# A second FFN with seven block products, GpSimd's queue for the block sums of the last FFN, and a chunk split from its head in the third FFN

## The chip, the cores and the metric

The kernel runs on one core of one Trainium2 chip. The metric is device time in microseconds (us). Every run has a time of its own; one execution was also recorded by the hardware profiler, and its span, from the first to the last instruction, is a little shorter than its time.

## What is computed

The reference is a trunk of two layers for 256 tokens of width 1024, in float32. Each layer is an FFN, a mixer and a second FFN, each behind an RMSNorm and added to the stream:

```python
def swiglu(x, w_gate, w_up, w_down):
    return (jax.nn.silu(x @ w_gate) * (x @ w_up)) @ w_down
...
        h = h + 0.5 * swiglu(rms_norm(h, ffn1_norm[layer]),
                             ffn1_w_gate[layer], ffn1_w_up[layer], ffn1_w_down[layer])
        hn = rms_norm(h, mix_norm[layer])
...
        h = h + 0.5 * swiglu(rms_norm(h, ffn2_norm[layer]),
                             ffn2_w_gate[layer], ffn2_w_up[layer], ffn2_w_down[layer])
    return rms_norm(h, final_norm)
```

There are four FFNs, 1024 wide outside and 2816 inside. The mixer of the first layer is dilated attention beside a gated MLP, that of the second is block-sparse attention; the change does not touch them.

## The kernel before

**Stages.** The work runs in six phases: FFN (phase 0), mixer (1), FFN (2), FFN (3), mixer (4), FFN (5). "First FFN" below is phase 0, "second" phase 2, "third" phase 3, "last" phase 5.

**A product is three matmuls.** Each float32 operand is split into a high part (rounded to the matmul's format) and a low part (the rest); `mm3` (lines 387 to 390) multiplies high by high, high by low and low by high. ACT makes the high part of a weight (`whi`, line 249), DVE the low part (`wlo`, line 256).

**Weights come in chunks.** `weight_chunks()` lists them in the order of use, mostly 1 MB: eight 128-row tiles of 256 columns. Class `Stream` loads them on SP's DMA queue into three buffers `raw` (line 201), splits them into four buffers `whi`/`wlo` and hands them to PE. So DVE and ACT can be at most four chunks ahead of PE: a chunk's split can begin when PE has left the chunk four places before it. A chunk with `reset=RESET` is split from a small head (the first three tiles, in two pieces of 384 columns) instead of in two halves of 1024.

**An FFN.** For each of 11 pairs of hidden tiles PE works one gate chunk and one up chunk, 48 matmuls each. Then `gated` (line 717) forms the hidden values: DVE multiplies the gate bank by the norm's row (`gs`, line 720), ACT takes the SiLU, DVE multiplies by the up bank (`hm`, line 723), and ACT and DVE split the result into `hTh` and `hTl` (line 393). Nothing can be gated until `everywhere` (lines 476 to 493) has summed the squares (`mean`, a square root on ACT, a reciprocal on DVE, `row`). The down projection follows: four groups of 256 output columns, each of three chunks (8, 8 and 6 tiles); `Next.pair` (line 430) takes a group out of its bank: `part` (437), `x` (438), then the split of the stream for the next phase, `xTh` and `xTl` (427).

**Seven products.** In the first FFN (`woven`) the first 512 columns of the down projection are made by seven block products instead of eight: the 256x256 block of hidden values and the 256x512 block of weights of a pair are cut in quarters, sums of quarters are formed, and `seven_products` (line 748) runs 7 x 3 matmuls on one chunk of kind "S" (0.5 MB). The sums of hidden quarters (`f` in `gated`, lines 738 to 740, split into `hSh` and `hSl`) and of weight quarters (lines 263, 266 and 267) are DVE's. They are worked `LAG` = 4 pairs behind the gating; the last four stand in the down projection. `gather_first` adds the seven results up, and `turned` (line 782) turns them round by four PE transposes for each 256 columns.

**Sums for the last FFN.** The last FFN uses the same trick with nine of its down chunks. Their weight sums are made early, in the second and third FFN, by `begin_sums` (line 657): fetch 1 MB from HBM into a buffer `blocks` (line 666), form the sums in place on DVE (lines 670 to 672, and 676 into `block` for five of them), write 1 MB (or 1 MB and 256 KB) back to HBM (line 682). Both transfers are issued by SP, in its queue behind the last weight load. `AHEAD` names the chunks (phase, n) after which a fetch is issued; the sums are issued one chunk later and the write two chunks later. There are two `blocks` buffers.

**The order.** Each engine has one instruction queue, worked in order. The order is fixed when the program is built by a scheduler, which places an instruction where it expects its inputs to be there; `issue_after` ties an instruction to another of the same engine.

Of the kernel before, what the change touches and what calls it, by code (L numbers as in the profile page):

```python
# [10 lines left out]
F32 = mybir.dt.float32  # L11
F32R = mybir.dt.float32r
# [8 lines left out]
FT = FF // 128  # L21
# [3 lines left out]
CH = 2048  # L25
# [20 lines left out]
SPARE = 2  # L46
AHEAD = [(phase, n) for phase in (2, 3) for n in (4, 8, 12, 16)] + [(3, 19)]

WOVEN = (0,)
LAG = 4  # L50
MSHIFT, HSHIFT = 16, 56
# [4 lines left out]
def weight_chunks():  # L56
# [10 lines left out]

    def ffn(name, layer, last=False, again=(2, 3), woven=False):
        first = len(chunks)
        wd = (f"{name}_w_down", layer)  # L70

        def seven(pair):
            add(wd, pair * 256, 2, 0, 512, MSHIFT, kind="S")

        for c in range(0, FF, 256):
            if len(chunks) == 0:
                for k in (0, 4):
                    add((f"{name}_w_gate", f"{name}_w_up", layer), k * 128, 4, c, c + 256, SHIFT,
                        (1, 2, 3) if k else (0.5, 1, 1.5, 2, 3))
                continue  # L80
            for m in ("gate", "up"):
                n = len(chunks)
                cuts = (6,) if first == 0 and n in again else ()
                cols((f"{name}_w_{m}", layer), c, 256, cuts,
                     RESET if n - first in again or woven and m == "gate" and c // 256 > LAG else 0)
            if woven and c // 256 >= LAG:
                seven(c // 256 - LAG)
        if last:
            for i in range(FT // 2):
                add(wd, i * 256, 2, 0, D, kind=LAST[i])  # L90
            return
        rest = list(range(FT // 2 - LAG, FT // 2)) if woven else []
        behind = woven
        if woven:
            seven(rest.pop(0))
        for c in range(512 if woven else 0, D, 256):
            for k, n in DOWN:
                add(wd, k * 128, n, c, c + 256, SHIFT, reset=RESET if behind else 0)
                behind = bool(rest)
                if rest:  # L100
                    seven(rest.pop(0))
# [6 lines left out]

    ffn("ffn1", 0, again=(2,), woven=0 in WOVEN)
    wab = ("ab_w_in", 0)  # L110
# [6 lines left out]
    mix(("ab_w_out", 0), MIX1)  # L117
    ffn("ffn2", 0, again=(2,), woven=2 in WOVEN)
    ffn("ffn1", 1, again=(), woven=3 in WOVEN)
    wc = ("c_w_in", 0)  # L120
# [225 lines left out]
def trunk(ctx: ExitStack, tc: tile.TileContext, a, out):  # L346
# [311 lines left out]
    def begin_sums(fp, n):  # L658
# [4 lines left out]
        j = st.chunks - FT // 2 + i  # L663
        t = fp.tile([128, CH], F32, name="blocks", bufs=2)
        with tc.issue_after(st.last.ins):
            nc.sync.dma_start(t, st.weights[j].rearrange("(p c) -> p c", p=128))
        b22, b12, b11, b21 = (t[:, i * 512 : (i + 1) * 512] for i in range(4))

        def sums():
            nc.vector.tensor_sub(b12, b22, b12)  # L670
            nc.vector.tensor_add(b11, b12, b11)
            nc.vector.tensor_sub(b21, b11, b21)
            formed = [t]
            if LAST[i] == "X":
                formed.append(fp.tile([128, 512], F32, name="block", bufs=1))
                nc.vector.tensor_sub(formed[1], b11, b22)

            def keep():
                st.sums[j] = [dram.tile(list(b.shape), F32, name=f"blocks{n}{m}") for m, b in enumerate(formed)]
                with tc.issue_after(st.last.ins):  # L680
                    for to, b in zip(st.sums[j], formed):
                        nc.sync.dma_start(to, b)

            return keep
# [3 lines left out]
    def ffn(phase):  # L688
        nonlocal nxt
        with tc.tile_pool(name="fp", bufs=1) as fp:  # L690
            hT = [fp.tile([128, FT, S], F32R, name=n) for n in ("hTh", "hTl")]
            last = phase == 5
            woven = phase in WOVEN
            if last:
# [23 lines left out]
            def gated(k, pg, pu):  # L718
# [16 lines left out]
                if woven:  # L735
# [4 lines left out]
                    nc.vector.tensor_add(f[:, 3], a12, f[:, 2])  # L740
                    summed[k // 2] = [fp.tile([128, 4 * 128 + LINE], F32R, name=m, bufs=LAG + 1)[:, HSHIFT : HSHIFT + 512]
                                        .rearrange("p (i c) -> p i c", i=4) for m in ("hSh", "hSl")]
# [50 lines left out]
            for n in range(FT):  # L793
# [13 lines left out]
                if (phase, n) in AHEAD:  # L807
                    ahead.append(begin_sums(fp, AHEAD.index((phase, n))))
                if (phase, n - 1) in AHEAD:
                    ahead.append(ahead.pop()())  # L810
                if (phase, n - 2) in AHEAD:
                    ahead.pop()()
# [16 lines left out]
                elif n > late and m == 1:  # L829
                    gated(k, *ready[-2:])  # L830
                if woven and m == 1 and k // 2 >= LAG:
                    seven_products(k // 2 - LAG)
            if last:
# [6 lines left out]
            nxt = Next(phase + 1)  # L840
            rest = list(range(FT // 2 - LAG, FT // 2)) if woven else []
            if woven:
                seven_products(rest.pop(0))
            for c in range(2 if woven else 0, 4):
                b = bank()
                for k0, n in DOWN:
                    w = st.take()
                    turns = [(j, kk) for kk in range(RESET, n) for j in range(2)]
                    for j, kk in [(j, kk) for j in range(2) for kk in range(RESET)] + turns:
# [3 lines left out]
                            k == j == 0, k == FT - 1 and j == 1)  # L853
                        if woven and c == 3 and k0 == 8 and j and kk in (3, 6):
                            turned(kk // 6, quarters[kk // 6])
# [600 lines left out]
```

## Time and profile before

| | |
|---|---|
| median of 3 runs | 922.58 us (922.55 to 923.53) |
| the profiled execution's own time | 922.25 us |
| its span | 920.5 us |
| first FFN, to 187 us | PE busy 186.17, DVE 168.18, ACT 119.39 |
| second FFN, 272 to 453 us | PE busy 181.00, DVE 126.42, ACT 92.77 |
| third FFN, 453 to 632 us | PE busy 179.00, DVE 124.06, ACT 87.30 |

A page of the profile gives, for each engine, the busy time, its waits with what ended them, and the chain of work that ended last. PE's matmuls overlap: one lasts about 0.28 us but the next starts 0.113 us after it, so that a busy PE is read by the distance between starts. "Pitch" below is that distance, for DVE's instructions too.

### The profile page before, as it was taken

The page shows a single profiled execution, that of the slowest core. Times are in us where ns is not written, and L with a number is a line of the kernel's source. Part 1 is how long each engine was busy: PE and PEld are TensorE (multiplying, and loading weights), DVE is VectorE, ACT ScalarE, POOL GpSimd, SP SyncE. Part 2 cuts the span into 40 slices and gives each one's busy share as a digit, 9 for nine tenths or more (in the row PEclk, how much of TensorE's full clock was granted, in tenths as well). Part 3 has the DMA queues.
Part 4 walks back from the last instruction along what each step waited for, and adds up shares of the span by engine and source line. Part 5 has one row for each costly group of instructions (what it writes and reads, how often), then busy time and mean ns, then how long its engine had stood idle before and what let it go on. Part 6 is the DMA issues. An engine that isn't in the chain of part 4 may idle for free.

```text
span 920.5 us, 18362 instructions
## 1 busy us (share of the span) xinstructions
PE 912.8 (99%) x7558; PEld 894.0 (97%) x7558; DVE 730.7 (79%) x1162; ACT 545.3 (59%) x840; POOL 82.1 (9%) x117
## 2 busy tenths in 40 slices
PE   9999999999999999999999999999999999999997
PEld 9999999989999999999999999999999999999886
DVE  7999897997889767655786677666778799878896
ACT  7766555668667544444564454355776777555574
POOL 0000000034310000000000000001565100000002
PEclk9999999999999999999999999999999999999999
DMA  9646555665256777765557877855433566755681
GB/s 331 244 163 239 201 177 204 231 227 183 93 184 229 245 276 266 288 236 214 205 207 271 294 255 295 323 210 199 177 138 138 134 228 223 271 201 194 230 310 54
DMA packets 34707, 202.17 MB, mean 220 GB/s; under 512 B 3984, under 2 KB 6288, under 8 KB 13760
## 3 DMA queue, kind: packets, MB, share of 16 engines
q1 hardware_dynamic: 33120, 197.79, 60.1%
q0 software_dynamic: 496, 1.77, 0.9%
q10 hardware_dynamic: 1008, 1.44, 0.5%
q8 instruction: 59, 0.97, 0.4%
q14 instruction: 24, 0.20, 0.1%
HBM read 188.14 MB, written 12.85 MB: 218 GB/s over the span
## 4 chain that ended last, share of the span: by engine, by line
PE 94%; issue 4%; DVE 1%; POOL 0%; ACT 0%; POOLq 0%; DVEq 0%
PE bank L388 30%; PE bank L389 30%; PE bank L390 30%; PE bank L636 1%; PE bank L1158 1%; DVE wlo L256 1%; PE bank L612 0%; PE bank L639 0%; POOL xTl L902 0%; PE bank L1120 0%; ACT whi L249 0%; PE bank L1122 0%; DVE xTl L427 0%; PE bank L1121 0%; DVE x L438 0%
## 5 line engine op out<-in xcount | busy, mean ns | idle before, releaser
L249 ACT ACTIVATE whi<-raw 128x1024 fp32r<-128x1024 f32 (+5 forms) x369 | 341.6, 970 | 244.0 <-PE bank L389 125.2
L256 DVE TENSOR_TENSOR wlo<-raw,whi 128x1024 fp32r<-128x1024 f32 (+5 forms) x369 | 402.8, 1120 | 56.3 <-ACT whi L249 55.2
L388 PE MATMUL bank<-xTh,whi 128*128 128x256 f32 x1600 | 442.7, 277 | 0.0
L389 PE MATMUL bank<-xTl,whi 128*128 128x256 f32 x1600 | 441.9, 276 | 0.3 <-DVE xTl L427 0.3
L390 PE MATMUL bank<-xTh,wlo 128*128 128x256 f32 x1600 | 441.8, 276 | 0.0
L389 PEld LDWEIGHTS bank<-xTl,whi 128*128 128x128 f32 x1600 | 300.4, 188 | 0.6 <-DVE xTl L427 0.5
L388 PEld LDWEIGHTS bank<-xTh,whi 128*128 128x128 f32 x1600 | 300.4, 188 | 0.0
L390 PEld LDWEIGHTS bank<-xTh,wlo 128*128 128x128 f32 x1600 | 300.4, 188 | 0.0
L388 PE MATMUL bank<-hTh,whi 128*128 128x256 f32 x440 | 121.7, 277 | 0.0
L390 PE MATMUL bank<-hTh,wlo 128*128 128x256 f32 x440 | 121.5, 276 | 0.0
L389 PE MATMUL bank<-hTl,whi 128*128 128x256 f32 x440 | 121.5, 276 | 0.0
L389 PEld LDWEIGHTS bank<-hTl,whi 128*128 128x128 f32 x440 | 82.6, 188 | 0.0
L388 PEld LDWEIGHTS bank<-hTh,whi 128*128 128x128 f32 x440 | 82.6, 188 | 0.0
L390 PEld LDWEIGHTS bank<-hTh,wlo 128*128 128x128 f32 x440 | 82.6, 188 | 0.0
L723 DVE TENSOR_TENSOR hm<-gs,bank 128x512 f32<-128x512 f32 x44 | 29.9, 683 | 34.8 <-PE bank L390 34.6
L1053 POOL MEMSET k<- 64x256 f32 x12 | 3.2, 306 | 563.7 <-ACT whi L249 378.9
L720 DVE TENSOR_TENSOR gs<-bank,row 128x512 f32<-128x512 f32 x44 | 30.1, 685 | 14.0 <-PE bank L390 13.9
L388 PE MATMUL bank<-mixh,whi 128*128 128x256 f32 x128 | 35.7, 279 | 0.0
L1149 POOL TENSOR_SCALAR pr<-pr,rl 128x128 f32<-128x128 f32 (+1 forms) x36 | 33.1, 931 | 28.2 <-DVE rl L1145 19.2
L390 PE MATMUL bank<-mixh,wlo 128*128 128x256 f32 x128 | 35.4, 277 | 0.0
L389 PE MATMUL bank<-mixl,whi 128*128 128x256 f32 x128 | 35.4, 276 | 0.0
L393 ACT ACTIVATE hTh<-hm 128x512 fp32r<-128x512 f32 x44 | 27.2, 619 | 10.4 <-DVE hm L723 9.5
(247 smaller groups left out, 1149.4 us busy)
## 6 DMA issues: line engine op xcount, KB each, us to landing
raw<-in_weights SPq DMA_DIRECT2D x135, 1024.0 KB, 5.0
blocks<-in_weights SPq DMA_DIRECT2D x9, 1024.0 KB, 9.3
blocks<-blocks SPq DMA_DIRECT2D x9, 1024.0 KB, 9.0
raw<-in_weights SPq DMA_DIRECT2D x17, 512.0 KB, 3.5
raw<-in_weights SPq DMA_DIRECT2D x10, 768.0 KB, 6.3
raw<-blocks SPq DMA_DIRECT2D x7, 1024.0 KB, 4.8
raw<-in_weights SPq DMA_DIRECT2D x7, 256.0 KB, 4.7
blocks<-block SPq DMA_DIRECT2D x5, 256.0 KB, 8.7
```

The costliest lines, as they stand in the source:

```text
L249: done = nc.scalar.activation(hi, r, AF.Copy)
L256: self.made[u] = done, nc.vector.tensor_sub(lo, r, hi.bitcast(F32))
L388: nc.tensor.matmul(p, sh, mh, start=start, stop=False)
L389: nc.tensor.matmul(p, sh, ml, start=False, stop=False)
L390: return nc.tensor.matmul(p, sl, mh, start=False, stop=stop)
L393: return nc.scalar.activation(hi, src, AF.Copy), nc.vector.tensor_sub(lo, src, hi.bitcast(F32))
L636: nc.tensor.matmul(o, w[0][i][:, cs], xT[m][:, k], start=k == 0 and m == "h" and j % 2 == 0, stop=False)
L720: nc.vector.tensor_mul(g, both(pg), twice(norm["row"]))
L723: nc.vector.tensor_mul(hm, g, both(pu))
L1053: nc.gpsimd.memset(pair[j][o, 1].bitcast(F32), 0.0)
L1149: share = engine.tensor_scalar(pr[:, cs], pr[:, cs], rl[:, b : b + 1], None, op0=ALU.mult)
L1158: nc.tensor.transpose(tp[:, i * 128 : (i + 1) * 128], pr[:, i * 128 : (i + 1) * 128], ident)
```

## The change

It does five things:

1. `WOVEN` and `LAG` become `LAGS = {0: 4, 2: 2}`: the second FFN too makes its first 512 down columns by seven products, two pairs behind the gating. Its last two pairs stand in the down projection, and `turned` stands one down chunk earlier than in the first FFN.
2. `begin_sums` issues its fetch and its writes on GpSimd's queue instead of SP's.
3. There is one `blocks` buffer instead of two.
4. The sums are issued two chunks behind their fetch and the write three, from other places (`AHEAD`).
5. In the third FFN the second chunk (the first up chunk) is split from its head.

```diff
-AHEAD = [(phase, n) for phase in (2, 3) for n in (4, 8, 12, 16)] + [(3, 19)]
-
-WOVEN = (0,)
-LAG = 4
+AHEAD = [(2, n) for n in (3, 7, 11, 15)] + [(3, n) for n in (2, 6, 10, 14, 18)]
+
+LAGS = {0: 4, 2: 2}
...
-            if woven and c // 256 >= LAG:
-                seven(c // 256 - LAG)
+            if c // 256 >= lag:
+                seven(c // 256 - lag)
...
-        if woven:
+        if lag > 2 and woven:
             seven(rest.pop(0))
...
-    ffn("ffn2", 0, again=(2,), woven=2 in WOVEN)
-    ffn("ffn1", 1, again=(), woven=3 in WOVEN)
+    ffn("ffn2", 0, again=(2,), phase=2)
+    ffn("ffn1", 1, again=(1,), phase=3)
...
-        t = fp.tile([128, CH], F32, name="blocks", bufs=2)
+        t = fp.tile([128, CH], F32, name="blocks", bufs=1)
         with tc.issue_after(st.last.ins):
-            nc.sync.dma_start(t, st.weights[j].rearrange("(p c) -> p c", p=128))
+            nc.gpsimd.dma_start(t, st.weights[j].rearrange("(p c) -> p c", p=128))
...
                 with tc.issue_after(st.last.ins):
                     for to, b in zip(st.sums[j], formed):
-                        nc.sync.dma_start(to, b)
+                        nc.gpsimd.dma_start(to, b)
...
-                if (phase, n - 1) in AHEAD:
+                if (phase, n - 2) in AHEAD:
                     ahead.append(ahead.pop()())
-                if (phase, n - 2) in AHEAD:
+                if (phase, n - 3) in AHEAD:
                     ahead.pop()()
...
-                        if woven and c == 3 and k0 == 8 and j and kk in (3, 6):
+                        if woven and (c, k0) == (3, 8 if lag > 2 else 0) and j and kk in (3, 6):
                             turned(kk // 6, quarters[kk // 6])
```

`issue_after(st.last.ins)` now stands around instructions of another engine than SP, so that it ties nothing. The places of the changed instructions in the engines' queues are shown here as the builder printed them.

SP's queue in the second FFN of the kernel before: the block transfers stand between the weight loads, and a write back waits there for DVE's sums. `raw` are weight chunks.

```order
L201 DMA raw_3911<-in_weights 128x2048
L666 DMA blocks_3913<-in_weights 128x2048
L201 DMA raw_3970<-in_weights 128x2048
L201 DMA raw_4037<-in_weights 128x2048
L682 DMA blocks00_4039<-blocks_3913 128x2048
L201 DMA raw_4096<-in_weights 128x2048
L201 DMA raw_4160<-in_weights 128x2048
L666 DMA blocks_4162<-in_weights 128x2048
```

GpSimd's queue (POOL) in the second FFN of the changed kernel, with what each transfer waits for (DMASW is the landing of one of GpSimd's own transfers); before, nothing stood here.

```order
L667 DMA blocks_4167<-in_weights 128x2048 [waits DMASW1_49]
L683 DMA blocks10_4436<-blocks_4167 128x2048 [waits DMASW2_49,DVE_49]
L667 DMA blocks_4498<-in_weights 128x2048 [waits DMASW3_49]
L683 DMA blocks20_4769<-blocks_4498 128x2048 [waits DMASW4_49,DVE_49]
L683 DMA blocks21_4770<-block_4665 128x512 [waits DVE_49]
L667 DMA blocks_4833<-in_weights 128x2048 [waits DMASW5_49]
```

SP's queue keeps the weight loads alone. Each fetch now waits for the landing of the write before it (there is one buffer), and each write for the fetch's landing and DVE's sums: the transfers are a chain.

DVE's queue in the third FFN of the kernel before, from the third sums of this FFN (`blocks_6474`) to the next gate (`wlo` are low parts of weight chunks):

```order
L670 TENSOR_TENSOR blocks_6474<-blocks_6474 128x512
L720 TENSOR_TENSOR gs_6663<-bank_6545,row_5783 128x512
L671 TENSOR_TENSOR blocks_6474<-blocks_6474 128x512
L256 TENSOR_TENSOR wlo_6595<-raw_6408,whi_6594 128x1024
L672 TENSOR_TENSOR blocks_6474<-blocks_6474 128x512
L676 TENSOR_TENSOR block_6536<-blocks_6474 128x512
L256 TENSOR_TENSOR wlo_6595<-raw_6408,whi_6594 128x1024
L723 TENSOR_TENSOR hm_6666<-gs_6663,bank_6606 128x512
L256 TENSOR_TENSOR wlo_6656<-raw_6472,whi_6655 128x1024 x2
L393 TENSOR_TENSOR hTl_5653<-hm_6666,hTh_5652 128x512
L720 TENSOR_TENSOR gs_6791<-bank_6670,row_5783 128x512
```

and of the changed kernel, from its fourth sums of this FFN (`blocks_6775`) to the fifth (`blocks_7028`) and the chunk behind them:

```order
L671 TENSOR_TENSOR blocks_6775<-blocks_6775 128x512
L672 TENSOR_TENSOR blocks_6775<-blocks_6775 128x512
L721 TENSOR_TENSOR gs_6458<-bank_6339,row_5952 128x512
L673 TENSOR_TENSOR blocks_6775<-blocks_6775 128x512
L257 TENSOR_TENSOR wlo_6389<-raw_6203,whi_6388 128x1024 x2
L677 TENSOR_TENSOR block_6901<-blocks_6775 128x512
L724 TENSOR_TENSOR hm_6461<-gs_6458,bank_6399 128x512
L257 TENSOR_TENSOR wlo_6449<-raw_6271,whi_6448 128x1024 x2
L394 TENSOR_TENSOR hTl_5822<-hm_6461,hTh_5821 128x512
L721 TENSOR_TENSOR gs_6581<-bank_6465,row_5952 128x512
L671 TENSOR_TENSOR blocks_7028<-blocks_7028 128x512
L257 TENSOR_TENSOR wlo_6515<-raw_6330,whi_6514 128x1024 x2
```

Before, about two pairs of the FFN lay between two sums; now the sums of the third FFN follow each other at every pair or less, from its first chunk on, and are over by the sixth of the 11 pairs. `wlo_6515` is the fifteenth chunk of this FFN.

DVE's queue in the second FFN of the changed kernel, up to the sums of hidden quarters (`hSl`) of the first pair, which the first seven-product chunk needs right behind the third pair's up chunk:

```order
L724 TENSOR_TENSOR hm_3854<-gs_3851,bank_3659 128x512
L724 TENSOR_TENSOR hm_3868<-gs_3865,bank_3790 128x512
L739 TENSOR_TENSOR gs_3851<-hm_3854 128x256
L739 TENSOR_TENSOR gs_3865<-hm_3868 128x256
L740 TENSOR_TENSOR gs_3851<-gs_3851,hm_3854 128x128
L740 TENSOR_TENSOR gs_3865<-gs_3865,hm_3868 128x128
L394 TENSOR_TENSOR hTl_3594<-hm_3854,hTh_3593 128x512
L741 TENSOR_TENSOR gs_3851<-hm_3854,gs_3851 128x128
L394 TENSOR_TENSOR hTl_3594<-hm_3868,hTh_3593 128x512
L741 TENSOR_TENSOR gs_3865<-hm_3868,gs_3865 128x128
L257 TENSOR_TENSOR wlo_3929<-raw_3714,whi_3928 128x1024
L394 TENSOR_TENSOR hSl_3862<-gs_3851,hSh_3861 128x512
```

In the kernel before, the same place (the `hm` of the first two pairs and the `hTl` behind them) read:

```order
L720 TENSOR_TENSOR gs_3842<-bank_3600,row_3781 128x512
L256 TENSOR_TENSOR wlo_3835<-raw_3655,whi_3834 128x1024 x2
L720 TENSOR_TENSOR gs_3849<-bank_3716,row_3781 128x512
L723 TENSOR_TENSOR hm_3845<-gs_3842,bank_3657 128x512
L723 TENSOR_TENSOR hm_3852<-gs_3849,bank_3785 128x512
L393 TENSOR_TENSOR hTl_3592<-hm_3845,hTh_3591 128x512
L720 TENSOR_TENSOR gs_3975<-bank_3856,row_3781 128x512
L256 TENSOR_TENSOR wlo_3906<-raw_3712,whi_3905 128x1024
L393 TENSOR_TENSOR hTl_3592<-hm_3852,hTh_3591 128x512
```

Six small rows for two pairs (`gs`, 256 and 128 wide) and one `hSl` per pair are new there.

More of the change, by code (lines that the diff above doesn't have):

```diff
@@ L66, in cols, with ffn @@
             add(m, k * 128, n, c0, c0 + w, SHIFT if w == 256 else 0, cuts, reset)
-    def ffn(name, layer, last=False, again=(2, 3), woven=False):
+    def ffn(name, layer, last=False, again=(2, 3), phase=None):
         first = len(chunks)
         wd = (f"{name}_w_down", layer)
+        lag = LAGS.get(phase, FT)
+        woven = phase in LAGS
         def seven(pair):
@@ L84, in ffn @@
                 cols((f"{name}_w_{m}", layer), c, 256, cuts,
-                     RESET if n - first in again or woven and m == "gate" and c // 256 > LAG else 0)
-            if woven and c // 256 >= LAG:
-                seven(c // 256 - LAG)
+                     RESET if n - first in again or woven and m == "gate" and c // 256 > lag else 0)
+            if c // 256 >= lag:
+                seven(c // 256 - lag)
         if last:
@@ L91, in ffn @@
             return
-        rest = list(range(FT // 2 - LAG, FT // 2)) if woven else []
+        rest = list(range(FT // 2 - lag, FT // 2)) if woven else []
         behind = woven
-        if woven:
+        if lag > 2 and woven:
             seven(rest.pop(0))
@@ L97, in ffn @@
             for k, n in DOWN:
-                add(wd, k * 128, n, c, c + 256, SHIFT, reset=RESET if behind else 0)
+                add(wd, k * 128, n, c, c + 256, SHIFT, reset=RESET if behind or woven and (c, k) == (768, 16) else 0)
                 behind = bool(rest)
@@ L692, in ffn @@
             last = phase == 5
-            woven = phase in WOVEN
+            lag, woven = LAGS.get(phase, FT), phase in LAGS
             if last:
@@ L740, in gated @@
                     nc.vector.tensor_add(f[:, 3], a12, f[:, 2])
[L741 removed]
+                    at = 0 if phase else HSHIFT
+                    summed[k // 2] = [fp.tile([128, 4 * 128 + LINE], F32R, name=m, bufs=lag + 1)[:, at : at + 512]
                                         .rearrange("p (i c) -> p i c", i=4) for m in ("hSh", "hSl")]
@@ L830, in ffn @@
                     gated(k, *ready[-2:])
-                if woven and m == 1 and k // 2 >= LAG:
-                    seven_products(k // 2 - LAG)
+                if m == 1 and k // 2 >= lag:
+                    seven_products(k // 2 - lag)
             if last:
@@ L840, in ffn @@
             nxt = Next(phase + 1)
-            rest = list(range(FT // 2 - LAG, FT // 2)) if woven else []
-            if woven:
+            rest = list(range(FT // 2 - lag, FT // 2)) if woven else []
+            if lag > 2 and woven:
                 seven_products(rest.pop(0))
```

2 lines of the change are left out of this document (1 added, 1 removed).

## The prediction

> **What bounds the kernel now.** I read the page first: the span, the busy times, the chain that ended last.
>
> ```profile
> span 920.5 us, 18362 instructions
> ...
> PE 912.8 (99%) x7558; PEld 894.0 (97%) x7558; DVE 730.7 (79%) x1162; ACT 545.3 (59%) x840; POOL 82.1 (9%) x117
> ...
> PE 94%; issue 4%; DVE 1%; POOL 0%; ACT 0%; POOLq 0%; DVEq 0%
> ```
>
> The chain runs through PE. A share over the whole span hides the stages, so next I cut the trace into windows: the second FFN, the third, and a stretch of the first, which already works with seven products. The columns are the stretch, its length, then busy time of PE, PEld, DVE, ACT and POOL with instruction counts, the granted clock, the DMA share and GB/s.
>
> ```profile
> 272.00:453.00 181.00, 181.00 (x1599) 181.00 (x1598) 126.42 (x152) 92.77 (x117) 0.00 (x0) 1.00 0.68 245
> 453.00:632.00 179.00, 179.00 (x1582) 179.00 (x1581) 124.06 (x148) 87.30 (x108) 0.00 (x0) 1.00 0.72 259
> 110.00:135.00 25.00, 25.00 (x222) 25.00 (x221) 22.63 (x35) 13.26 (x19) 0.00 (x0) 1.00 0.50 171
> ```
>
> PE has no hole in either FFN that the change touches. Where seven products are already used, DVE is busy for 22.63 of 25 us and PE still has no hole. The granted clock is 1.00 in each. Third, PE's waits (who waited for whom, total, times, longest):
>
> ```profile
> PE bank L612 <- PEq L1443: 0.8, 1, 0.8
> PE bank L389 <- DVE xTl L427: 0.3, 1, 0.3
> ```
>
> That is all that PE waits. So a gain must come from fewer or shorter PE instructions; every other edit can only cost, or cost nothing. How much delay the other engines can take before PE feels it, the waits of ACT show:
>
> ```profile
> ACT whi L249 <- PE bank L389: 125.2, 58, 3.4
> ```
>
> ACT waits for PE to give back a weight buffer: the splits run the full four chunks ahead. A chunk is 48 matmuls.
>
> **PE's work.** A pair of the down projection's first 512 columns took 8 products of 3 matmuls and now takes 7. Over 11 pairs that is 264 matmuls before and 231 after, 33 fewer. Their pitch, and the price of `turned`, from the first FFN's own transposes:
>
> ```profile
> 175.09 0.60 PE L787 MATMUL bank<-ident,hm 128*128 128x128 f32 x4
> 175.45 0.37 PE L388 MATMUL bank<-hTh,whi 128*128 128x256 f32 x1
> 175.66 0.28 PE L389 MATMUL bank<-hTl,whi 128*128 128x256 f32 x1
> ```
>
> Pitch: 25.00 us over 222 matmuls above gives 0.1126 with the window's edges; single steps in the timeline are 0.11 or 0.12, and I use 0.1134. 33 x 0.1134 = 3.74 us go. From 175.09 to 175.66 are four transposes and one matmul: 0.57 - 0.11 = 0.46 us; two such groups add 0.91. Net on PE: **-2.83 us**.
>
> **DVE in the second FFN, steady part.** Here stand the new rows of `gated` (256, 128 and 128 wide, then `hSl`) and the weight sums, as in the first FFN:
>
> ```profile
> 108.79 0.68 DVE L720 TENSOR_TENSOR gs<-bank,row 128x512 f32<-128x512 f32 x1
> ...
> 113.58 0.69 DVE L723 TENSOR_TENSOR hm<-gs,bank 128x512 f32<-128x512 f32 x1 [1.84 <-PE bank L390]
> ...
> 115.15 0.42 DVE L738 TENSOR_TENSOR gs<-hm 128x256 f32<-128x256 f32 x1
> 115.48 1.22 DVE L256 TENSOR_TENSOR wlo<-raw,whi 128x1024 fp32r<-128x1024 f32 x1
> 116.62 0.69 DVE L393 TENSOR_TENSOR hTl<-hm,hTh 128x512 fp32r<-128x512 f32 x1
> 117.22 0.28 DVE L739 TENSOR_TENSOR gs<-gs,hm 128x128 f32<-128x128 f32 x1
> 117.43 0.55 DVE L256 TENSOR_TENSOR wlo<-raw,whi 128x384 fp32r<-128x384 f32 x1
> 117.89 0.28 DVE L740 TENSOR_TENSOR gs<-hm,gs 128x128 f32<-128x128 f32 x1
> ...
> 122.09 0.68 DVE L720 TENSOR_TENSOR gs<-bank,row 128x512 f32<-128x512 f32 x1
> ```
>
> One pair is 122.09 - 108.79 = 13.30 us, of which 1.84 is waiting for PE: DVE needs 11.46. PE needs (48 + 48 + 21) x 0.1134 = 13.27. The block sums add 3 or 4 rows of 512 (0.60 each, 116.62 to 117.22) at every second pair: 2.4 more on 2 x 11.46 = 25.3 against 26.5. DVE stays below PE, so nothing is charged. The cover is thin: 1.2 us in two pairs.
>
> **The start of the second FFN** is where lag 2 matters. The first seven-product chunk stands behind the third pair's up chunk, and needs `hSl`. DVE cannot gate before `row` is there, so three pairs come at once:
>
> ```profile
> 285.22 0.41 DVE L393 TENSOR_TENSOR accl<-acc,acch 128x256 fp32r<-128x256 f32 x1
> ...
> 292.77 1.75 DVE L485 RECIPROCAL inverse<-sqrt 128x256 f32<-128x256 f32 x1 [0.32 <-ACT sqrt L484]
> ...
> 295.93 0.69 DVE L720 TENSOR_TENSOR gs<-bank,row 128x512 f32<-128x512 f32 x1
> ...
> 305.72 0.69 DVE L723 TENSOR_TENSOR hm<-gs,bank 128x512 f32<-128x512 f32 x1 [0.76 <-PE bank L390]
> ```
>
> The third pair's up chunk ends at 305.7, when this `hm` is released. PE's next matmul starts about 0.2 us earlier, 305.5, and the ninth of the new chunk, the first that reads `hSl`, at 305.5 + 8 x 0.1134 = 306.4. By the new order DVE has, between `accl` and that `hSl`, 11 rows of 512, 10 of 256, 4 of 1024, the reciprocal (1.78), one each of 768 and 1280, two of 384 and four of 128. With pitches of 0.60, 0.33, 1.13 and 0.21 from the rows above (0.46 for 384; 0.87 and 1.40 in proportion) and 0.4 for rows that wait for the row ahead of them, that is 20.6 us; waiting for ACT's square root adds 0.6 (0.32 shown). 285.2 + 21.2 = 306.4 starts `hSl`, which takes 0.7: ready at 307.1 to 307.3. PE waits **+0.9 us**. The bounds: 0, since 0.9 is under a twentieth of the rows that I added up; 2.5, if one more 1024 row (1.13) and another wait for ACT (0.3) come first.
>
> **The tail of the second FFN.** With two seven-product chunks in the down projection DVE is fuller when `xTl` is due. The first FFN's tail is the nearest row:
>
> ```profile
> 186.98 0.87 DVE L427 SCALAR_TENSOR_TENSOR xTl<-x,gT,xTh 128x256 fp32r<-128x256 f32 x2
> ```
> ```profile
> 186.89 0.28 PE L388 MATMUL bank<-xTh,whi 128*128 128x256 f32 x1
> 187.51 0.39 PE L389 MATMUL bank<-xTl,whi 128*128 128x256 f32 x1 [0.35 <-DVE xTl L427]
> ```
>
> There PE lost 0.62 - 0.11 = 0.5 us. In the new order fewer splits stand ahead of `xTl`, and by the same pitches it comes 0.7 to 1.1 us before PE asks. I take 0; bound 0.5.
>
> **The head in the third FFN** replaces two `wlo` of 1024 by pieces of 384, 384 and 1280: one row more, 0.2 us of DVE, within 179.00 - 124.06 = 55 us of idle time. Cost 0; a gain is excluded since PE has no hole there.
>
> **The queues.** SP loses 9 fetches and 14 writes. Before, the loads behind a write stood in SP's queue until DVE's sums were made. PE never felt that, so nothing is gained. POOL's queue has nothing else in these FFNs (0.00 busy). DVE already waits for fetches, without PE noticing:
>
> ```profile
> DVE blocks L670 <- DMA blocks<-in_weights: 26.8, 9, 4.9
> ```
>
> But with one buffer the transfers are a chain: a fetch waits for the landing of the write before it. The trace has no 1 MB transfer from GpSimd's queue. The nearest rows: the same 1 MB from SP while no blocks move (400 to 480 us) and while they do (480 to 560), and the same 192 KB from both kinds of queue (columns: KB each, us to landing):
>
> ```profile
> raw<-in_weights SPq DMA_DIRECT2D x14, 1024.0 KB, 4.9
> ```
> ```profile
> raw<-in_weights SPq DMA_DIRECT2D x13, 1024.0 KB, 7.2
> blocks<-in_weights SPq DMA_DIRECT2D x4, 1024.0 KB, 9.6
> blocks<-blocks SPq DMA_DIRECT2D x3, 1024.0 KB, 9.0
> ```
> ```profile
> xn<-in_final_norm POOLq DMA_DIRECT2D x1, 512.0 KB, 5.8
> ...
> mask<-in_consts ACTq DMA_DIRECT2D x1, 192.0 KB, 3.8
> mask<-in_consts POOLq DMA_DIRECT2D x1, 192.0 KB, 4.7
> ```
>
> With one block transfer in flight at a time, beside a load: 4.9 + 0.9 (the `mask` difference) + 0.6 for sharing = 6.4 us for a fetch, F, and 13 for a round of write and fetch, R. Bounds: 4.9 and 9.8 (as SP's loads alone), 9.6 and 18.6 (as SP's block transfers). I take 6.4 because the 9.6 and 9.0 came when up to three transfers shared the engines. In the second FFN the new order puts 11 to 12 us of DVE rows between the second, third and fourth sums, so with R = 13 DVE waits 1 to 2 us at each, inside its lead over PE (7 us or more there by the same count); PE would feel it from R of about 16. The third FFN comes first.
>
> **Where the chain decides.** The fetch there waits for the second FFN's last `x`:
>
> ```profile
> 452.33 0.28 PE L388 MATMUL bank<-xTh,whi 128*128 128x256 f32 x1
> ```
> ```profile
> 453.25 0.69 DVE L438 TENSOR_TENSOR x<-part,x 128x512 f32<-128x512 f32 x1
> ```
>
> 1.6 us after PE's first matmul of the third FFN, so it is issued at 1.7 (time now counts from that matmul). Five fetches, of which four go back through a round: the ninth sum's data is there at 1.7 + F + 4R + 14.1. The 14.1 are DVE's rows between a landing and the sum that the write waits for (4.1, 5.3, 1.8, 2.4 by the new order and the pitches) and 0.5 of steps between engines. In DVE's order the ninth sum stands ahead of `wlo_6515`, the fifteenth chunk. One sum row and half the split take 1.7 more. PE asks for it with its third matmul, at 14 x 48 x 0.1134 + 0.2 = 76.4. PE waits F + 4R - 58.9: for 6.4 and 13 that is -0.5, just in time, **0 us**. It is a close thing: the lead of four chunks, 21 us, is used up.
>
> **Sum.** 922.25 - 2.83 + 0.9 + 0 + 0 = 920.3 for an execution like the profiled one. The median of before is 0.33 above that execution; so **920.6**, 0.2% less. About 0.2% (1.85 us) is also what a measurement of this kernel can tell from no change.
>
> **Rivals.**
>
> *The chain is late (slower).* With F = 7 and R = 14 PE waits 7 + 56 - 58.9 = 4.1 us; with 7.5 and 15, 8.6; with the upper bound, 9.6 + 74.4 - 58.9 = 25. The time: 920.6 + 4.1 = 924.7, or 929.2. It decides from R = 13.1 on, with some 4.5 us for each us of R. For it: 512 KB from POOL's queue took 5.8, and doubled for 1 MB nearer 7.5 than 6.4; raw loads took 7.2 in the stretch with blocks. Against it: one transfer at a time puts less on the engines than the old pairs. Chance 0.30.
>
> The Trainium skill, "DMA: Bandwidth & Descriptors", section "Measured (HBM→SBUF, 128 partitions, SWDGE, issued from GpSimd)", gives 6.15 us for 1 MB with the issue and the completion left out; with some 2 us around it, an estimate from that page, the fetch would be near 8 and PE would wait about 13 us, a time of 934. Its section on the anatomy of such a transfer fits 2.0 us plus bytes over 436 GB/s, 4.4 us for 1 MB, by which nothing waits; the two do not agree. No row here shows a 1 MB transfer of that kind.
>
> *Everything is covered.* `hSl` comes in time and the chain too: 922.25 - 2.83 + 0.33 = 919.75. For it: the 0.9 us is a difference of two sums of twenty rows. Chance 0.13.
>
> *The second FFN is tighter on DVE.* The start costs 2.5 and the tail 0.5: 922.25 - 2.83 + 3.0 + 0.33 = 922.75. For it: three pairs are gated in 20 us with no slack. Against it: the splits recover 1.8 us in each pair. Chance 0.12.
>
> *The change does not do what it says.* The sums are to be formed two chunks behind their fetch, but `issue_after` ties them to nothing, and the new order has the third FFN's sums at every pair or less instead of every second. It is this that makes the chain tight; were they spread over two pairs each, R could be 21 (192 x 0.1134) and nothing would wait. This is fact, not chance, and is inside the cases above.
>
> **How the numbers follow.** The forecast case (919.6 to 922) has 0.45. Faster than 920.7: all of the covered case and 0.27 of the forecast's 0.45, 0.40. Slower than 924.4: most of the late chain, 0.26. The rest, 0.34. The range begins at 919.4, the covered case less 0.35 for the pitch, and ends at 927.5, a late chain with R = 14.7; some 0.13 lies above it, some 0.05 below.
>
> **What would show it.** PE's count falls by 25 (33 - 8). In the second FFN PE waits once for `hSl` (or `hSh`) near 306, about 0.9 us, and nowhere else. The landing times of the `blocks` transfers on POOL's queue: 6 to 7 us confirms F, 8 or more means that the chain is late. Then DVE's waits for `blocks` in the third FFN grow to tens of us, and PE waits for `wlo` near 76 us into it. If PE waits inside the second FFN at every second pair, my count of DVE's rows is wrong; a wait at the second FFN's end points to `xTl`. If PE's waits are those two alone and the time is still over 921, the PE pitch or a cost outside these two FFNs is what I missed.

## The result

The changed kernel takes 932.71 us (median of 4 runs, 929.91 to 934.79), against 922.58 before: a ratio of 1.0105, 95% interval 1.0093 to 1.0118. It is slower by 10 us where 920.6 was forecast, and lies above the range.

The page of the profile after, its span, the busy times and the chain that ended last:

```profile
span 930.0 us, 18498 instructions
...
PE 916.5 (99%) x7533; PEld 896.9 (96%) x7533; DVE 770.9 (83%) x1270; ACT 561.0 (60%) x876; POOL 94.3 (10%) x140
...
PE 85%; DMA 8%; DVE 5%; issue 2%; ACT 0%; SPq 0%; POOLq 0%; POOL 0%; DVEq 0%
```

PE has its 25 instructions less. But DMA, which was not in the chain, now holds 8% of it. The waits of PE (who waited for whom, total, times, longest):

```profile
PE bank L391 <- DVE wlo L257: 5.0, 2, 4.2
PE bank L613 <- PEq L1445: 0.8, 1, 0.8
PE bank L391 <- DVE hSl L394: 0.7, 1, 0.7
PE bank L637 <- ACT whi L250: 0.4, 1, 0.4
```

Two rows were not there before: one for `hSl`, which the prediction charged, and one for `wlo` with two waits, where it had looked at one and called it "just in time". Their places on PE's timeline (start, duration, and in brackets the idle time and its releaser):

```profile
307.24 0.28 PE L390 MATMUL bank<-wlo,hSh 128*128 128x256 f32 x1
308.25 0.39 PE L391 MATMUL bank<-whi,hSl 128*128 128x256 f32 x1 [0.73 <-DVE hSl L394]
...
520.25 0.28 PE L390 MATMUL bank<-xTl,whi 128*128 128x256 f32 x1
521.40 0.39 PE L391 MATMUL bank<-xTh,wlo 128*128 128x256 f32 x1 [0.87 <-DVE wlo L257]
...
532.29 0.28 PE L390 MATMUL bank<-xTl,whi 128*128 128x256 f32 x1
536.73 0.58 PE L391 MATMUL bank<-xTh,wlo 128*128 128x256 f32 x1 [4.16 <-DVE wlo L257]
```

Start to start, less one pitch: 1.01 - 0.11 = 0.9 us for `hSl`; 1.15 - 0.12 = 1.0 and 4.44 - 0.11 = 4.3 for `wlo`, of the thirteenth and of the fifteenth chunk of the third FFN. Together 6.2 us. With the 2.83 us that PE saves, the span should have grown by 3.4, to 924. It grew by 9.5. So waits alone don't explain it, and the next view is one that the prediction never used on PE: how many matmuls fit into a stretch of equal length. The windows, of after (columns as before; the x behind PE's time is its count, the 1.00 or 0.50 the granted clock):

```profile
458.00:518.00 60.00, 60.00 (x511) 60.00 (x511) 36.89 (x46) 25.75 (x31) 4.31 (x8) 1.00 0.74 279
...
536.80:540.10 3.30, 3.30 (x15) 3.30 (x16) 3.27 (x5) 0.00 (x0) 0.60 (x2) 0.50 0.36 82
```

and the first of them in the kernel before:

```profile
458.00:518.00 60.00, 60.00 (x532) 60.00 (x531) 43.15 (x50) 31.57 (x39) 0.00 (x0) 1.00 0.70 251
```

PE is "busy" for 60 of 60 us in both, at a granted clock of 1.00 in both, and does 511 matmuls in the one and 532 in the other. The distance between starts is 0.1178 us instead of 0.1133, from 457.9 us on, until the wait at 520 ended it: a few matmuls behind that wait, at 522, it is 0.1133 again. Shorter stretches of 0.1178 lie at 5 to 17, 176 to 189, 274 to 285, 307 to 311 and 442 to 449 us. In all that is 110 us, of which 3.8% is lost, 4.2 us; the profile of before has no such stretch outside its mixers. And behind the 4.2 us wait the clock is granted at 0.50 for 3.4 us: 15 matmuls in place of 29, 1.6 us.

The sum, from before to after: -2.83 (fewer instructions) + 0.9 (`hSl`) + 5.3 (`wlo`) + 1.6 (half the clock) + 4.2 (long pitch) + 0.4 (ACT's `whi` at the start) - 0.5 (before's wait for `xTl`, gone) = 9.1, of 9.5 measured.

### The profile page after: what moved, and what is told of

Its sections match the earlier page's. It is cut to its first block, busy times and chain, and to the rows that moved or that the text cites. A ratio compares the mean times of both kernels' runs of the same rounds, so it can differ in the third digit from the quotient of the medians.

```text
span 930.0 us, 18498 instructions
## 1 busy us (share of the span) xinstructions
PE 916.5 (99%) x7533; PEld 896.9 (96%) x7533; DVE 770.9 (83%) x1270; ACT 561.0 (60%) x876; POOL 94.3 (10%) x140
## 4 chain that ended last, share of the span: by engine, by line
PE 85%; DMA 8%; DVE 5%; issue 2%; ACT 0%; SPq 0%; POOLq 0%; POOL 0%; DVEq 0%
PE bank L391 27%; PE bank L389 27%; PE bank L390 27%; DMA blocks<-in_weights 4%; DMA blocks<-blocks 2%; DVE wlo L257 2%; DMA raw<-in_weights 1%; PE bank L1160 1%; PE bank L637 1%; PE bank L640 0%; DVE xTl L428 0%; DVE blocks L673 0%; DVE x L435 0%; ACT whi L250 0%; PE bank L1122 0%
## 5 line engine op out<-in xcount | busy, mean ns | idle before, releaser
L389 PE MATMUL bank<-hTh,whi 128*128 128x256 f32 x352 | 98.0, 278 | 0.0
L391 PE MATMUL bank<-hTh,wlo 128*128 128x256 f32 x352 | 97.6, 277 | 0.0
L390 PE MATMUL bank<-hTl,whi 128*128 128x256 f32 x352 | 97.6, 277 | 0.0
L389 PEld LDWEIGHTS bank<-hTh,whi 128*128 128x128 f32 x352 | 66.2, 188 | 0.0
L390 PEld LDWEIGHTS bank<-hTl,whi 128*128 128x128 f32 x352 | 66.1, 188 | 0.0
L722 ACT ACTIVATE gs<-gs 128x512 f32<-128x512 f32 x44 | 27.4, 624 | 46.0 <-DVE gs L721 45.8
L394 ACT ACTIVATE hSh<-gs 128x512 fp32r<-128x512 f32 (+1 forms) x31 | 18.6, 601 | 36.1 <-DVE gs L741 18.5
L389 PE MATMUL bank<-whi,hTh 128*128 128x256 f32 (+1 forms) x114 | 36.1, 317 | 0.0
L390 PE MATMUL bank<-wlo,hTh 128*128 128x256 f32 (+1 forms) x114 | 36.1, 317 | 0.0
L391 PE MATMUL bank<-whi,hTl 128*128 128x256 f32 (+1 forms) x114 | 36.1, 317 | 0.0
```

The costliest lines, as they stand in the source:

```text
L389: nc.tensor.matmul(p, sh, mh, start=start, stop=False)
L390: nc.tensor.matmul(p, sh, ml, start=False, stop=False)
L391: return nc.tensor.matmul(p, sl, mh, start=False, stop=stop)
L394: return nc.scalar.activation(hi, src, AF.Copy), nc.vector.tensor_sub(lo, src, hi.bitcast(F32))
L722: nc.scalar.activation(g, g, AF.Silu)
```

## The experiments

Two causes stand beside each other: the chain of transfers behind the waits, and the long pitch, which begins with the chunk that the change splits from a head. Rivals were that DVE has too many rows whatever the chain does, and that POOL's transfers slow PE down. Every ratio below is to the kernel before on the same chip, with its 95% interval.

**Sums tied.** The sums get a place in DVE's queue by a tie to the newest split:

```diff
+            with tc.issue_after(st.made[max(st.made)][1].ins):
                 nc.vector.tensor_sub(b12, b22, b12)
                 nc.vector.tensor_add(b11, b12, b11)
                 nc.vector.tensor_sub(b21, b11, b21)
```

> The changed kernel with each block sum tied on DVE behind the split of the chunk that is newest where the sum is written, so that sums stand four chunks apart instead of two or three; queue, single buffer and head as in the change. Theory (the late chain of transfers made PE wait 5.6 us, and the half clock that followed 4.3 us of it cost 1.7 more; the pitch of 0.118 us is the head's doing): no wait of PE for wlo in the third FFN, no half clock; but the slow pitch, which in the changed kernel was ended by the wait, now lasts to the end of the third FFN, 180 us at 3.9% = 6.8 us instead of 2.4: 932.7 - 7.3 + 4.4 = about 930. Rival (DVE has too many rows, whatever the chain does): PE still waits 3 to 6 us for wlo, 932 or more. Rival (POOL's transfers slow PE's pitch): the pitch is slow while they run and recovers behind the last, about 927 to 928.

Measured: 927.60 us (927.20 to 927.99), ratio 1.0053 (1.0041 to 1.0065), some 2 us under the number expected: the wait for `hSl` went too (0.9), and the sum was made from the median, 1.0 above the execution that was accounted for. PE waits for DVE nowhere; DVE waits for no block. That is the first theory, and against the rival of too many rows: the same rows are all still there. The long pitch now runs on to the second mixer. The windows of the third FFN in this run:

```profile
460.00:636.00 176.00, 176.00 (x1497) 176.00 (x1495) 117.61 (x138) 81.61 (x100) 7.01 (x13) 1.00 0.67 246
```

**No head.**

```diff
-    ffn("ffn1", 1, again=(1,), phase=3)
+    ffn("ffn1", 1, again=(), phase=3)
```

> The changed kernel without the head in the third FFN; all else the same. Theory (head makes the slow pitch, chain makes the wait): the third FFN runs at 0.1133 from its start, PE comes to the fifteenth chunk 2.4 us sooner, and waits so much longer for the same transfers: 8 us of waiting in place of 5.6, the time within 1 us of the change's 932.7. Rival (POOL's transfers slow the pitch): the pitch stays at 0.118 from 458 to 520 and the waits stay at 5.6, 932.7 too, but told apart by the pitch. Rival (the head's rows are what delays DVE): waits shrink, 930 or less.

Measured: 931.49 us (928.19 to 938.50), ratio 1.0107 (1.0078 to 1.0136). The pitch in the third FFN is 0.1133, and no clear gain is left: the runs lie 10 us apart, so that the number decides little, and the trace has to. PE's waits in this run:

```profile
PE bank L391 <- DVE wlo L257: 5.5, 2, 4.2
PE bank L391 <- DVE hSl L394: 1.3, 1, 1.3
```

The two waits for `wlo` are 1.4 and 4.4 us from start to start, 0.5 more than with the head, where 2.4 were expected. PE came to them at nearly the same times as with the head (519.96 and 532.37 us against 520.25 and 532.29), since its third FFN began 2.1 us later in this run (454.34 against 452.27): it had lost 1.8 us to waits for `hSh` and `hSl` instead of 0.9, and more to half a clock behind them. Half a clock stands at two places here, 3.4 us behind the wait for `hSl` and 6.8 us from the last wait for `wlo` on.

**Both.**

> Both: the sums tied and no head. Theory: no wait in the third FFN, no half clock, pitch 0.1133 there: 932.7 - 7.3 - 2.4 = about 923.0, and down to 921 if the short slow stretches elsewhere (at the start, near 176, 274 and 442 us; 1.7 us in all) do not come again. Rival (DVE overloaded by the seven products of the second FFN): waits remain, 926 or more. Rival (POOL's transfers slow the pitch): 0.118 in the third FFN while they run, 927.

Measured: 920.34 us (919.91 to 921.07, 9 runs), ratio 0.9977 (0.9968 to 0.9987): faster than both kernels, and 0.7 under the least that was expected. Like that of the tied run, the expectation was worked out from the median, and left the wait for `hSl` in. PE's only wait left is the one at the start. The same window as above:

```profile
460.00:636.00 176.00, 176.00 (x1556) 176.00 (x1555) 123.31 (x146) 85.83 (x108) 9.65 (x22) 1.00 0.69 254
```

1556 matmuls where the run with tied sums and the head had 1497, with POOL's transfers running in both: they are not what makes the pitch long.

**The head by itself**, in the kernel before:

```diff
-    ffn("ffn1", 1, again=(), woven=3 in WOVEN)
+    ffn("ffn1", 1, again=(1,), woven=3 in WOVEN)
```

> The kernel before with the head in the third FFN and nothing else of the change. Theory (the head turns the pitch to 0.118 when it is entered at 0.113, and nothing in the third FFN turns it back): 0.118 from 458 us to the mixer's first head near 640, 6.8 us more, 929.4. Rival (the slow pitch needs POOL's transfers): 922.6, no change. Rival (the head's own rows cost PE nothing and the pitch falls by chance): a spread between 922.6 and 929.4 over the runs.

Measured: 929.62 us (928.98 to 930.14), ratio 1.0074 (1.0062 to 1.0086). The head alone costs 7.3 us. Around its chunk, whose first matmul is at 457.54, the steps of the timeline go from 0.11 to 0.12 and stay there until 645.7 us, where four matmuls of one column and the mixer's first head follow:

```profile
457.31 0.28 PE L389 MATMUL bank<-xTl,whi 128*128 128x256 f32 x1
457.43 0.28 PE L390 MATMUL bank<-xTh,wlo 128*128 128x256 f32 x1
457.54 0.28 PE L388 MATMUL bank<-xTh,whi 128*128 128x256 f32 x1
457.66 0.28 PE L389 MATMUL bank<-xTl,whi 128*128 128x256 f32 x1
457.78 0.28 PE L390 MATMUL bank<-xTh,wlo 128*128 128x256 f32 x1
457.89 0.28 PE L388 MATMUL bank<-xTh,whi 128*128 128x256 f32 x1
```

```profile
460.00:636.00 176.00, 176.00 (x1497) 176.00 (x1496) 116.77 (x138) 81.09 (x100) 0.00 (x0) 1.00 0.70 253
```

The changed kernel has 27 heads in its FFNs, and 25 behave otherwise: nine matmuls at about 0.1175 (they read the first halves of the head's three tiles, which the kernel puts at word 52 of a line of 64 words, and all others at word 16: `RESHIFT` and `SHIFT`), then 0.1133 again. They even end a long pitch that came before: in the second FFN of the changed kernel the one of 274 us ends behind the head at 284.3. What is different at this one? Ahead of 24 of the heads stands another kind of matmul: a seven-product chunk, a small product with `ident`, or, in the second and the last FFN, a matmul of a single column that the kernel issues for nothing else. Ahead of this one stands a plain chunk. (The two others behind a plain chunk, at 179.5 and at 448 us, are told of below.)

**The head behind a one-column matmul**, in the kernel before with the head:

```diff
+                if phase == 3 and n == 0:
+                    nc.tensor.matmul(bank()[:, :1], ones, ones[:, :1], start=True, stop=True)
```

> The kernel before with the head in the third FFN (as in only_head, 929.6) and one matmul of a single column issued ahead of that head's chunk, as the kernel has it already ahead of the heads of the second and the last FFN. Theory (a head that is entered straight from a plain chunk leaves PE at 0.118 us, one that is entered behind another kind of matmul goes back to 0.113, as the 30-odd heads of the changed kernel's trace do): the third FFN runs at 0.113, 922.5. Rival (it is the place or the data of this chunk): it stays at 0.118, 929.8.

Measured: 922.74 us (922.09 to 923.46, 10 runs), ratio 1.0004 (0.9995 to 1.0012): the whole cost is gone. The added matmul on the timeline (its two parts in one row), and the third FFN:

```profile
458.11 0.28 PE L390 MATMUL bank<-xTh,wlo 128*128 128x256 f32 x1
458.22 0.28 PE L808 MATMUL bank<-ones 128*128 128x1 f32 x2
458.36 0.36 PE L388 MATMUL bank<-xTh,whi 128*128 128x256 f32 x1
```

```profile
460.00:636.00 176.00, 176.00 (x1555) 176.00 (x1555) 121.80 (x144) 85.81 (x106) 0.97 (x4) 1.00 0.71 261
```

**The head one chunk later** (`again=(2,)`).

> The kernel before with a head at the third chunk of the third FFN (the second gate chunk) in place of the second chunk, again straight behind a plain chunk. Theory (what stands ahead of a head decides): 0.118 from 463 us on, 929.4. Rival (the second chunk is special): 0.113, 922.3.

Measured: 929.85 us (929.27 to 929.95), ratio 1.0077 (1.0064 to 1.0090), with the long pitch from 463.5, the head's first matmul, to 645.8 us:

```profile
463.30 0.28 PE L481 MATMUL bank<-acch,all_ones 128*128 128x256 f32 x1
463.42 0.28 PE L482 MATMUL bank<-accl,all_ones 128*128 128x256 f32 x1
```

```profile
460.00:636.00 176.00, 176.00 (x1498) 176.00 (x1497) 116.90 (x138) 81.45 (x101) 0.00 (x0) 1.00 0.70 254
```

So it isn't the second chunk that is special. But this head is not straight behind a plain chunk, as the expectation has it: the two products of `everywhere` with `all_ones` stand between, as wide as any other (256 columns), and do not keep the pitch short. In the third FFN what stands ahead of a head decides, and it is not enough that it is something else than a weight chunk.

**The transfers by themselves**: the change without seven products in the second FFN and without the head (`LAGS = {0: 4}`, `again=()`).

> The kernel before with the change's second, third and fourth part alone: GpSimd's queue, one buffer, sums two chunks behind their fetch; no seven products in the second FFN, no head. The builder orders the sums as early as in the change, or earlier. Theory (the chain alone makes the wait): PE waits for wlo in the third FFN by 5 to 10 us, with half a clock behind it: 922.3 + 6 to 12 = 928 to 934; no wait for hSl near 306. Rival (it takes the second FFN's added rows on DVE to make the chain late): under 924.

Measured: 932.93 us (930.97 to 941.22), ratio 1.0126 (1.0097 to 1.0154). PE waits for `wlo` in the second FFN too, at 344.5, and there is no wait for `hSl`:

```profile
PE bank L391 <- DVE wlo L257: 3.9, 2, 2.5
PE bank L613 <- PEq L1445: 0.8, 1, 0.8
```

The chain alone makes PE wait, as the theory had it, but the waits are shorter than its 5 to 10 us: 1.5 us at 344.5 and 2.7 at 538.6, from start to start. Behind the first of them the pitch is long from 346 to 539 us, until the second ends it, without any head: 192 us, 7.3 us of time, more than the waits themselves. The time is inside the range expected by another sum than the one expected, and that is luck. Waits can turn the pitch either way.

**The seven products by themselves**: the change with `nc.sync` in place of `nc.gpsimd` at the three transfers, and no head.

> The changed kernel with all block transfers on SP's queue again and no head: the first part of the change, with one buffer and the new places of fetch and sum. SP's queue holds the transfers in order between the weight loads, and the sums stand four or five chunks apart. Theory: no wait in the third FFN; 33 matmuls less 8 transposes, 922.3 - 2.8 + 0 to 0.9 = 919.5 to 920.4, the same as tied_no_head (920.3), so that GpSimd's queue as such gives nothing. Rival (one buffer is late on any queue): PE waits for wlo in the third FFN, 924 or more. Rival (GpSimd's queue frees SP's and so helps): 921.5 or more, through waits for raw.

Measured: median 922.52, but in two groups: seven runs from 920.68 to 922.85 and five from 927.27 to 929.61; ratio 1.0016 (0.9995 to 1.0037). No wait for the chain: one buffer on SP's queue is in time. The profiled run is of the upper group. Its pitch is long from 455.4 to 644.5 us, and what turned it is this wait, too short for the list of waits (0.17 instead of 0.11 from start to start):

```profile
455.16 0.28 PE L389 MATMUL bank<-xTh,whi 128*128 128x256 f32 x1
455.27 0.34 PE L390 MATMUL bank<-xTl,whi 128*128 128x256 f32 x1
455.44 0.28 PE L391 MATMUL bank<-xTh,wlo 128*128 128x256 f32 x1
455.56 0.28 PE L389 MATMUL bank<-xTh,whi 128*128 128x256 f32 x1
```

0.06 us of waiting for the last `xTl` of the second FFN, and 7 us behind it, in this one profile.

**The same with the head and the one-column matmul.**

> seven_alone (all block transfers on SP's queue, one buffer) with the head in the third FFN and the one-column matmul ahead of it. seven_alone had two groups of times, 920.7 to 922.9 and 927.3 to 929.6, and its profile, of the upper group, shows PE at 0.118 us from 455.4 us on, behind a wait of 0.06 us for xTl. Theory (that wait, by chance, turns the pitch, and nothing in the third FFN turns it back; a head behind a one-column matmul does): one group of times, 921 to 923, no run above 925. Rival (something else, such as loads on SP's queue, makes the upper group): the upper group stays.

Measured: 922.58 us (920.23 to 925.64, 11 runs), ratio 0.9998 (0.9988 to 1.0008). The group above 927 is gone. In the profiled run, of 920.67 us, PE waits for the same `xTl` by a little, and the third FFN runs at 0.1133:

```profile
454.61 0.36 PE L390 MATMUL bank<-xTl,whi 128*128 128x256 f32 x1
454.81 0.28 PE L391 MATMUL bank<-xTh,wlo 128*128 128x256 f32 x1
```

In this run a second such wait, at 455.04 us, has brought 0.1133 back before the head's chunk begins, so that the profile doesn't show the head end a long pitch here; that no run of 11 lies above 927, where 5 of 12 did, is what speaks for the theory. Its number was missed: the runs still spread over 5 us, one is above 925, and the median is no lower. What is in those runs stays open.

**The whole change, mended**: tied sums, and the one-column matmul ahead of the head.

> The whole change with the two mends: the sums tied (as in tied) and the one-column matmul ahead of the third FFN's head. Theory: 920.3 (tied_no_head) + 0.2 for the matmul + 0.1 for the head's nine slow matmuls = 920.5 to 920.8. Rival (the head's extra rows on DVE are felt once the chain is mended): PE waits in the third FFN, 922 or more.

Measured: 920.92 us (920.37 to 921.88, 11 runs), ratio 0.9982 (0.9973 to 0.9991). The whole change is 1.7 us faster than before, once its sums and its head are set right. The version without the head has 920.34, so that the head gains nothing even so.

## Why the prediction was wrong

**Right in the count, nearly in time: PE's work.** 25 instructions fewer, as forecast. With both causes taken away (sums tied, no head) the second FFN takes 177.9 us from its first matmul to that of the third, against 180.0 before: 2.1 less, where 2.83 was forecast. 0.3 of the rest is the long pitch at 440 to 448 us. The sum had no term for the nine slower matmuls of the new heads in this FFN (below); 11 heads x 9 x 0.0042 us is an estimate of 0.4.

**Right, the size in part by luck: the start of the second FFN.** 0.9 us of waiting for `hSl` was forecast near 306, and 0.9 at 307.2 was measured. In the run without the head, which has the same second FFN, it was 0.4 for `hSh` and 1.5 for `hSl`. In the tied runs it is gone: the first block sum, which the new order had put between `accl` and `mean`, stands behind `hSl` there.

**Wrong in size: the chain.** The step that failed is "I take 6.4" for a fetch F, with the rows between a landing and the next issue behind it, and from them "just in time, 0 us". The issues of the third FFN's transfers on POOL's timeline (the first fetch, the last two and the write between them), the landing of the last as DVE's sum met it, and the transfers of this stretch (KB each, median us to landing):

```profile
454.54 0.55 POOL L667 DMA_DIRECT2D blocks<-in_weights  x1 [83.55 <-ACT whi L250]
...
507.83 0.54 POOL L667 DMA_DIRECT2D blocks<-in_weights  x1 [2.65 <-DMA blocks<-blocks]
520.50 0.53 POOL L683 DMA_DIRECT2D blocks<-blocks  x1 [12.13 <-DVE blocks L673]
...
525.17 0.55 POOL L667 DMA_DIRECT2D blocks<-in_weights  x1 [1.24 <-DMA blocks<-blocks]
```

```profile
534.85 0.69 DVE L671 TENSOR_TENSOR blocks<-blocks 128x512 f32<-128x512 f32 x1 [7.70 <-DMA blocks<-in_weights]
535.46 2.35 DVE L257 TENSOR_TENSOR wlo<-raw,whi 128x1024 fp32r<-128x1024 f32 x2
```

```profile
raw<-in_weights SPq DMA_DIRECT2D x12, 1024.0 KB, 7.0
blocks<-in_weights POOLq DMA_DIRECT2D x5, 1024.0 KB, 9.5
blocks<-blocks POOLq DMA_DIRECT2D x5, 1024.0 KB, 6.4
```

The prediction had the data of the ninth sum 1.7 + 6.4 + 4 x 13 + 14.1 = 74.2 us after PE's first matmul of the third FFN (452.27 here). The sum met it at 82.6, 8.4 later. One by one, from issue to landing, the five fetches took 5.4, 7.2, 9.5, 9.7 and 9.6 us and the four writes between them 6.8, 6.4, 4.1 and 4.4: 63.1 in all instead of 58.4, which is 4.7 of the 8.4. The fetches are 9.4 over their sum and the writes 4.7 under, so that the round R came out at 13.4, near the 13 that was taken, and the last fetch at 9.6. DVE's rows between a landing and the next issue, with the steps between engines, took 17.2 instead of 14.1 (3.1): each of the four groups of rows was 0.5 to 0.7 longer, and 0.3 went by from each write's landing to the next fetch, where 0.5 had been taken for all such steps together. The start was 0.6 late. PE felt 5.3 of it, because 0.5 was to spare and its own pitch had become longer. The first wait, of 1.0 us, stands behind the sum before the last, where the prediction charged nothing.

The mechanism, the place of the larger wait (`wlo` of the fifteenth chunk) and the way of working it out were those of the rival "the chain is late", which had 0.30. (The upper end of the range, 927.5, belongs to R = 14.6 in that working, not 14.7.) What sized F wrongly is the 0.6 "for sharing" in 4.9 + 0.9 + 0.6, which no row showed: the first fetch took 5.4 and the last three some 4 us more. I set the two slower rows, 9.6 for a fetch beside loads and 7.2 for a raw load in the same stretch, aside as the effect of three transfers at a time. With one 1 MB block transfer at a time (a write of 256 KB still ran beside two of the five fetches) the loads still took 7.0 there and the fetch 9.5. In the second FFN 1 MB took 6.8 and the write 5.6 (medians), and in the tied run, whose sums are further apart, a fetch of the third FFN took 6.6 and a load 5.1. Why the fetches were slow with the sums close together was not tested by itself.

The Trainium skill, "DMA: Bandwidth & Descriptors", section "Measured (HBM→SBUF, 128 partitions, SWDGE, issued from GpSimd)", gives 6.15 us for 1 MB; with some 2 us around it, the prediction's estimate from it, 8 us, lies between the medians of 6.8 and 9.5 us that this trace shows for a fetch. The 4.4 us of the fit in the Trainium skill's section on the anatomy of a transfer is below each of the nine fetches (5.1 to 9.7 us).

**Missed: half the clock.** The wait of 4.2 us cost 1.6 us more, by the granted clock of 0.50 in the 3.4 us behind it. The Trainium skill, "TensorE: Matmul & The Clock Gate", section "Part 1: The HAM clock gate (the 'warmup' mystery)", says that an idle window of about 3.4 us halves PE's clock, and that it takes such a window of work to come back: 3.4 us is what this trace shows. Single waits of 1.0 us (at 520), 1.4 us (no head, at 520) and 1.5 us (the transfers by themselves, at 344.5) had no such effect. But one of 2.7 us (the transfers by themselves, at 538.6) had it, and in the run without the head one of 1.5 us, with another of 0.4 just ahead of it, at 307. A rule of one whole idle window, as the Trainium skill states it in that section, would give neither.

**Wrong: the head.** The second step that failed is "Cost 0; a gain is excluded since PE has no hole there", which looked for holes only. The head left no hole and took no time on DVE that anybody waited for; it changed the distance between matmuls, by 4%, for all that came behind it, 2.4 us in the changed kernel and 7.3 where nothing ends it. That the one-column matmul ahead of other heads belonged to them was in the code to be seen. The forecast's last sentence, that a longer pitch would be what is missed if waits don't explain the time, named the view but gave it no chance.

**Left out: other heads.** With seven products the second FFN also gets heads at eight gate chunks and three down chunks that stand behind a seven-product chunk. And the diff gives one to the last down chunk of each FFN with seven products. Neither the list of changes nor the prediction has them:

```diff
-                add(wd, k * 128, n, c, c + 256, SHIFT, reset=RESET if behind else 0)
+                add(wd, k * 128, n, c, c + 256, SHIFT, reset=RESET if behind or woven and (c, k) == (768, 16) else 0)
```

In the second FFN the last one ends, at 449, the long pitch that began at the transposes. In the first it stands at 179.5 straight behind a plain chunk. In the changed kernel the pitch is long there already, from the transposes at 176 on, and this head doesn't end it; in the tied run and in the run without the head it is 0.1133 up to this head and long from it on. In every profiled run that has this head the pitch is long from about 179 to 188 us, 9 us or more (0.3 to 0.5 us of time); in the profiles of before and of the runs made from it, it is not.

**Right by accident: the tail.** 0 was charged, with a bound of 0.5, and in the changed kernel `xTl` is in time. On SP's queue it is late by 0.06 us in the profiled run, and that costs 7 us through the pitch. A bound on a wait is no bound on what it sets off.

**Not decided.** Why a head that is entered behind a plain chunk, or behind the two 256-column products of `everywhere`, leaves PE at 0.1178, and one behind a one-column matmul or a seven-product chunk (256 columns, too) at 0.1133. In the third FFN it was so each time. But the head at 448 us of the changed kernel, also straight behind a plain chunk, is entered at 0.1178 and ends the long pitch, and the one at 179.5 is entered at 0.1178 too and doesn't. GpSimd's queue against SP's, with the sums in nearly the same places, is 920.92 against 922.58 us (tied with the head and the one-column matmul, and the seven products with them): intervals that just overlap, and a cause that was not looked for.

## What to carry to other kernels

A single buffer that is filled, worked and written back is a chain; its round is the sum of its latencies under the load of that stage and of every row and step between them, and the latency that counts is read in the busiest stretch, not in the calm one. Where PE is without holes, compare how many matmuls fit into equal windows of two traces before trusting "busy 100%": a pitch 4% longer shows in no list of waits. And an edit that a scheduler turns into another order should be read in that order: here a tie that no longer tied let the sums move ahead, and putting one back, on the right engine, was worth 5 us with the head and 11 without it.

## What the runs showed of the hardware

- PE has two steady distances between 256-column matmuls of this kind, 0.1133 and 0.1178 us, at the same granted clock of 1.00. It changes from one to the other at a wait, be it of 0.06 us (455.3, the seven products by themselves), at transposes (176 and 442, the changed kernel), or at the nine first matmuls of a head (457.5, the head by itself), and then stays there, for up to 190 us.
- A matmul of one column, 0.2 us, ahead of such a head was enough to have the short distance behind them (922.74 against 929.62 us).
- The granted clock fell to 0.50, for 3.4 or 6.8 us, behind PE waits of 2.7 to 4.4 us and once behind two of 0.4 and 1.5 us close together; it stayed at 1.00 behind single waits of 1.0, 1.4 and 1.5 us.
